# A load and three stores cut into halves of 64 partitions, and wider matmuls on zeros, in a 3x3 convolution

## The chip, the cores and the metric

The kernel runs on one core of one Trainium2 chip. The metric is device time in microseconds (us). A profile is that of a single execution; its span, from the first to the last instruction, is mostly some 1.8 us shorter than the time. A run counts as slow when it is over 1.5% above the fastest of its kernel; only fast runs are compared.

## The reference

A dense convolution, although nine tenths of the weights are zero: 16 images of 64 channels and 64x64 pixels, f32, padded by one, to 128 channels.

```python
x = randn(16, 64, 64, 64);  weight = randn(128, 64, 3, 3) * (random > 0.9)
for b, co, ci, kh, kw:
    output[b, co] += weight[co, ci, kh, kw] * x_pad[b, ci, kh:kh+64, kw:kw+64]
```

Input is 16.8 MB, output 33.6 MB.

## The kernel before

Two images form a pair: 2 x 64 channels fill the 128 partitions of one x tile. Eight pairs are computed one after the other. GpSimd issues the loads of x, which cast f32 to bf16 on the way. The first 32 rows of pair 0 come another way: SyncE loads them as f32, so that they land sooner (at 6.81 us; the cast load of the other 32 rows, issued 0.06 us later, lands at 8.75), and VectorE and ScalarE cast them. TensorE waits for these rows and does matmuls on zeros meanwhile, to keep its clock up (in head_halves, below, they end too soon, and the clock row falls to 5).

```python
x_head = o_pool.tile([128, H, W], FP32, name="o")
nc.sync.dma_start(out=x_head[:, 0:HEAD, :], in_=pair(0)[:, 0:HEAD, :])        # HEAD = 32 rows
nc.gpsimd.dma_start(out=xs[0][:, HEAD:H, :], in_=pair(0)[:, HEAD:H, :])
ident = const_pool.tile([128, 128], BF16, name="ident")
make_identity(nc, ident)
for p in range(1, EARLY):            # pairs 1 to 3, then 24 rows of pair 4
    load(p)
load(EARLY, 0, CUT)
idle_rhs = const_pool.tile([128, 128], BF16, name="idle_rhs")
def keep_busy(n):
    for _ in range(n):
        nc.tensor.matmul(idle_ps, idle_rhs, idle_rhs, start=True, stop=True)
keep_busy(27)
# ... weights cast and transposed ...
keep_busy(28)
# ...
for p in range(NP):                  # the eight pairs
    # ... matmuls, sums; a later pair's load is issued after the pair's last block ...
            if last and blk % 2 == 1:        # the last pair goes in four parts
                for n in range(2):
                    rows = slice(r0 - 16, r0 + 16)
                    nc.sync.dma_start(out=out[2 * p + n][:, rows, :], in_=o[n][:, rows, :])
        if not last:
            for n in range(2):
                nc.sync.dma_start(out=out[2 * p + n], in_=o[n])       # one image, 2 MB
```

SyncE issues all stores. Its DMAs take eight completion semaphores in turn, 0 to 7, and at the end SyncE waits for all eight in that order.

Of the kernel before, what the change touches and what calls it, by code (L numbers as in the profile page):

```python
# [8 lines left out]
FP32 = mybir.dt.float32  # L9
BF16 = mybir.dt.bfloat16  # L10
# [17 lines left out]
def kernel(  # L28
# [6 lines left out]
    nc = tc.nc  # L35
# [5 lines left out]
    HEAD = 32  # L41

    const_pool = ctx.enter_context(tc.tile_pool(name="const", bufs=1))
# [4 lines left out]
    psum_pool = ctx.enter_context(  # L48
        tc.tile_pool(name="psum", bufs=8, space=bass.MemoryType.PSUM)
    )  # L50
# [4 lines left out]
    def pair(p):  # L55
        return x[2 * p : 2 * p + 2].rearrange("n i h w -> (n i) h w")
# [2 lines left out]
    w_sb = const_pool.tile([C_OUT, C_IN * KH * KW], FP32, name="w_sb")  # L59
    nc.sync.dma_start(out=w_sb, in_=weight.rearrange("o i kh kw -> o (i kh kw)"))  # L60
    x_head = o_pool.tile([128, H, W], FP32, name="o")
    nc.sync.dma_start(out=x_head[:, 0:HEAD, :], in_=pair(0)[:, 0:HEAD, :])
    nc.gpsimd.dma_start(out=xs[0][:, HEAD:H, :], in_=pair(0)[:, HEAD:H, :])  # L63
    ident = const_pool.tile([128, 128], BF16, name="ident")
    make_identity(nc, ident)
# [1 line left out]
    def load(p, a=0, b=H):  # L67
        nc.gpsimd.dma_start(out=xs[p][:, a:b, :], in_=pair(p)[:, a:b, :])  # L68
# [6 lines left out]
    load(EARLY, 0, CUT)  # L75


    idle_rhs = const_pool.tile([128, 128], BF16, name="idle_rhs")
    nc.vector.memset(idle_rhs, 0.0)  # L79
    idle_ps = psum_pool.tile([128, 128], FP32, name="ps")  # L80

    def keep_busy(n):
        for _ in range(n):
            nc.tensor.matmul(idle_ps, idle_rhs, idle_rhs, start=True, stop=True)  # L84

    keep_busy(27)



# [8 lines left out]
    def cast_x(copy, a, b):  # L98
        copy(out=xs[0][:, a:b, :], in_=x_head[:, a:b, :])  # L99
# [24 lines left out]
    nc.vector.tensor_copy(out=wT[:, G0], in_=ps0)  # L124
    ps2 = transposed(G2)
    nc.scalar.copy(out=wT[:, G2], in_=ps2)
    keep_busy(28)
    cast_x(nc.scalar.copy, 9, 18)
    difference(G01, ps0)
    difference(G21, ps2)  # L130
# [26 lines left out]
    def direct(p, o, r0, rows):  # L157
        ps = product(
            [(xs[p], G1, r0, 1), (xs[p], G0, r0 - 1, 1), (xs[p], G2, r0 + 1, 1)], rows
        )  # L160
        nc.scalar.copy(out=o[0][:, r0 : r0 + rows, :], in_=ps[0])  # L161
        nc.vector.tensor_copy(out=o[1][:, r0 : r0 + rows, :], in_=ps[1])  # L162

    def twos(p, o, r0):
        t0 = r0 // 2
        s = s_pool.tile([128, 8, W], BF16, name="s")
        nc.gpsimd.tensor_tensor(  # L167
            out=s, in0=xs[p][:, r0 : r0 + 16 : 2, :], in1=xs[p][:, r0 + 1 : r0 + 16 : 2, :], op=ADD
        )
        shared = product([(s, G1, 0, 1)], 8)  # L170
        pc = []
        for n in range(2):
            c = p_pool.tile([128, 8, W], FP32, name="pc")
            nc.scalar.copy(out=c, in_=shared[n])  # L174
            pc.append(c)
        even = [(xs[p], G21, r0 + 1, 2), (xs[p], G0, r0 - 1, 2)]
        odd = [(xs[p], G01, r0, 2), (xs[p], G2, r0 + 2, 2)]
        for first, terms in ((r0, even), (r0 + 1, odd)):
            ps = product(terms, 8)
            for n in range(2):  # L180
                nc.vector.tensor_tensor(  # L181
                    out=o[n][:, first : r0 + 16 : 2, :], in0=ps[n], in1=pc[n], op=ADD
                )

    for p in range(NP):
        o = [o_pool.tile([C_OUT, H, W], FP32, name="o") for _ in range(2)]
        last = p == NP - 1
        for blk in range(4):
            r0 = 16 * blk
            if BLOCKS[p][blk] == "T":  # L190
                twos(p, o, r0)


                if p == 1 and blk == 3:
                    load(EARLY, CUT, H)
                elif p > 1 and blk == 3 and p + EARLY - 1 < NP:
                    load(p + EARLY - 1)
            else:
                for r, rows in ((r0, 8), (r0 + 8, 8)):
                    direct(p, o, r, rows)  # L200
            if last and blk % 2 == 1:
                for n in range(2):
                    rows = slice(r0 - 16, r0 + 16)
                    nc.sync.dma_start(out=out[2 * p + n][:, rows, :], in_=o[n][:, rows, :])
        if not last:
            for n in range(2):
                nc.sync.dma_start(out=out[2 * p + n], in_=o[n])


# [28 lines left out]
```

## Time and profile before

| | before |
|---|---|
| time | 126.42 us (126.32 to 126.64, 3 runs) |
| span of the profile | 124.7 us |
| DMA, mean of the span | 344 GB/s of bytes written; 406 GB/s of HBM traffic |
| first rows land | 6.81 us |
| TensorE begins its convolution | 7.35 us |
| first store issued | 21.83 us |
| last store's 16 shares land | 120.98 to 123.59 us |
| from the last landing to the end | 1.16 us |

All DMAs run on 16 DMA engines; each engine carries one share of a DMA, and the semaphore rises by one as each share lands. So a DMA has 16 landings, and the last of them counts: those of the last store lie between 120.98 and 123.59 us, and SyncE's wait for them ends at 123.607. A second view, the chain that ended last, shows the way to TensorE's start (start, length, what):

```profile
1.18 5.63 DMA o<-in_x_dram
6.81 0.02 issue
6.83 0.47 DVE x L99
7.30 0.04 issue
7.35 102.09 PE ps L148 x954
```

The first rows' load, a cast of 0.47 us, then TensorE without a pause.

### The profile page before, as it was taken

The page shows a single profiled execution, that of the slowest core. Times are in us where ns is not written, and L with a number is a line of the kernel's source. Part 1 is how long each engine was busy: PE and PEld are TensorE (multiplying, and loading weights), DVE is VectorE, ACT ScalarE, POOL GpSimd, SP SyncE. Part 2 cuts the span into 40 slices and gives each one's busy share as a digit, 9 for nine tenths or more (in the row PEclk, how much of TensorE's full clock was granted, in tenths as well). Part 3 has the DMA queues.
Part 4 walks back from the last instruction along what each step waited for, and adds up shares of the span by engine and source line. Part 5 has one row for each costly group of instructions (what it writes and reads, how often), then busy time and mean ns, then how long its engine had stood idle before and what let it go on. Part 6 is the DMA issues. An engine that isn't in the chain of part 4 may idle for free.

```text
span 124.7 us, 2543 instructions
## 1 busy us (share of the span) xinstructions
PE 109.0 (87%) x1030; PEld 59.5 (48%) x1030; DVE 82.3 (66%) x135; ACT 39.0 (31%) x71; POOL 41.1 (33%) x46
## 2 busy tenths in 40 slices
PE   6999999999999999999999999999999999940000
PEld 6755555555555555555555555555555555510000
DVE  0354777877787778777877787778777878870000
ACT  4545323333333333333333333333333333300000
POOL 6427343533353335333533333333333300000000
PEclk9999999999999999999999999999999999998555
DMA  4999999999999999999999999999999999999991
GB/s 127 356 225 213 215 218 213 211 400 311 350 409 410 318 297 344 436 310 323 302 433 310 318 315 423 420 449 420 426 431 420 436 426 441 415 412 420 428 381 53
DMA packets 4188, 42.93 MB, mean 344 GB/s; under 512 B 464, under 2 KB 464, under 8 KB 976
## 3 DMA queue, kind: packets, MB, share of 16 engines
q1 hardware_dynamic: 2880, 34.90, 66.6%
q0 software_dynamic: 1296, 7.86, 30.8%
q8 instruction: 8, 0.13, 0.4%
q14 instruction: 4, 0.03, 0.1%
HBM read 17.07 MB, written 33.55 MB: 406 GB/s over the span
## 4 chain that ended last, share of the span: by engine, by line
PE 82%; DMA 5%; DVE 1%; issue 1%; DVEq 0%; SPq 0%
PE ps L148 82%; DMA o<-in_x_dram 5%; DVE o L181 1%; DVEq L233 0%; DVE x L99 0%; SPq L60 0%; DVEq L181 0%
## 5 line engine op out<-in xcount | busy, mean ns | idle before, releaser
L181 DVE TENSOR_TENSOR o<-ps,pc 128x512 f32<-128x512 f32 x124 | 77.8, 686 | 22.1 <-PE ps L148 19.8
L148 PE MATMUL ps<-x,wT 64*128 64x504 bf16 (+3 forms) x780 | 88.7, 373 | 0.3 <-DVE x L99 0.3
L148 PEld LDWEIGHTS <-wT 64*128 64x128 bf16 x966 | 54.4, 94 | 48.9 <-issue 0.3
L167 POOL TENSOR_TENSOR s<-x 128x512 bf16<-128x512 bf16 x31 | 35.6, 1151 | 57.5 <-PE ps L148 43.2
L174 ACT COPY pc<-ps 128x512 f32<-128x512 f32 x62 | 33.3, 589 | 64.0 <-issue 61.8
L148 PE MATMUL ps<-s,wT 64*128 64x512 bf16 (+1 forms) x186 | 25.7, 377 | 0.0
L84 PE MATMUL ps<-idle_rhs 128*128 128x128 bf16 x55 | 4.8, 265 | 1.0 <-DVE idle_rhs L79 1.0
L84 PEld LDWEIGHTS <-idle_rhs 128*128 128x128 bf16 x55 | 4.4, 123 | 1.0 <-DVE idle_rhs L79 1.0
L68 POOL DMA_DIRECT2D x<-in_x_dram x8 | 4.4, 561 | 0.0
L103 DVE CAST w_bf<-w_sb 128x192 bf16<-128x192 f32 (+1 forms) x4 | 1.1, 346 | 2.9 <-DMA w_sb<-in_weight_dram 2.9
L162 DVE COPY o<-ps 128x512 f32<-128x512 f32 x2 | 1.4, 692 | 2.0 <-PE ps L148 2.0
L161 ACT COPY o<-ps 128x512 f32<-128x512 f32 x2 | 1.2, 586 | 2.4 <-PE ps L148 2.4
L99 ACT CAST x<-o 128x576 bf16<-128x576 f32 (+1 forms) x2 | 1.5, 804 | 0.8 <-DMA o<-in_x_dram 0.8
L99 DVE CAST x<-o 128x576 bf16<-128x576 f32 x1 | 0.5, 460 | 1.9 <-DMA o<-in_x_dram 1.9
L103 ACT ACT_TABLE_LOAD x1 | 1.3, 1283 | 0.7 <-PEq L222 0.7
L109 PE MATMUL ps<-ident,w_bf 128*128 128x128 bf16 x9 | 1.1, 296 | 0.3 <-DVE w_bf L103 0.3
L103 ACT CAST w_bf<-w_sb 128x64 bf16<-128x64 f32 (+1 forms) x2 | 0.7, 416 | 1.8 <-DMA w_sb<-in_weight_dram 1.8
L109 PEld LDWEIGHTS <-w_bf 128*128 128x128 bf16 x9 | 0.8, 128 | 0.7 <-DVE w_bf L103 0.7
L113 DVE TENSOR_TENSOR wT<-ps,wT 128x384 bf16<-128x384 f32 x2 | 1.0, 548 | 0.0
L63 POOL DMA_DIRECT2D x<-in_x_dram x1 | 0.7, 693 | 0.8 <-POOLq L222 0.8
L79 DVE MEMSET idle_rhs<- 128x64 uint32 x1 | 0.1, 112 | 0.8 <-PEq L222 0.8
L122 ACT CAST wT<-ps 128x384 bf16<-128x384 f32 x1 | 0.5, 480 | 0.4 <-PE ps L109 0.4
(8 smaller groups left out, 2.0 us busy)
## 6 DMA issues: line engine op xcount, KB each, us to landing
out_dram<-o SPq DMA_DIRECT2D x14, 2048.0 KB, 17.4
x<-in_x_dram POOLq DMA_DIRECT2D x6, 1024.0 KB, 15.8
out_dram<-o SPq DMA_DIRECT2D x4, 1024.0 KB, 11.4
o<-in_x_dram SPq DMA_DIRECT2D x1, 1024.0 KB, 5.6
x<-in_x_dram POOLq DMA_DIRECT2D x1, 640.0 KB, 14.0
x<-in_x_dram POOLq DMA_DIRECT2D x1, 512.0 KB, 7.5
x<-in_x_dram POOLq DMA_DIRECT2D x1, 384.0 KB, 24.6
w_sb<-in_weight_dram SPq DMA_DIRECT2D x1, 288.0 KB, 3.0
```

The costliest lines, as they stand in the source:

```text
L68: nc.gpsimd.dma_start(out=xs[p][:, a:b, :], in_=pair(p)[:, a:b, :])
L84: nc.tensor.matmul(idle_ps, idle_rhs, idle_rhs, start=True, stop=True)
L99: copy(out=xs[0][:, a:b, :], in_=x_head[:, a:b, :])
L103: copy(out=w_bf4[:, g, a:b, :], in_=w_v[:, k : k + b - a, :])
L109: nc.tensor.matmul(wps[:, j, :], src, ident, start=True, stop=True)
L113: nc.vector.tensor_tensor(out=wT[:, g], in0=wps, in1=wT[:, G1], op=SUB)
L148: nc.tensor.matmul(ps[n][:, lo:hi, c_lo:c_hi], tap(g, kw, n), src[q, a:b:step, c_lo + kw - 1 : c_hi + kw - 1], start=(i == 0), stop=(i == ...
L161: nc.scalar.copy(out=o[0][:, r0 : r0 + rows, :], in_=ps[0])
L162: nc.vector.tensor_copy(out=o[1][:, r0 : r0 + rows, :], in_=ps[1])
L167: nc.gpsimd.tensor_tensor(out=s, in0=xs[p][:, r0 : r0 + 16 : 2, :], in1=xs[p][:, r0 + 1 : r0 + 16 : 2, :], op=ADD)
L174: nc.scalar.copy(out=c, in_=shared[n])
L181: nc.vector.tensor_tensor(out=o[n][:, first : r0 + 16 : 2, :], in0=ps[n], in1=pc[n], op=ADD)
```

## The change

The intent: 20 DMAs leave the last store on semaphore 3, and SyncE then walks through the waits for 4 to 7. With 24 the last store has semaphore 7. The four more DMAs come from cutting one load and three stores into two halves of 64 partitions. Besides, 55 narrow matmuls on zeros become 14 wide ones.

```diff
-    nc.sync.dma_start(out=x_head[:, 0:HEAD, :], in_=pair(0)[:, 0:HEAD, :])
+    for q in (slice(0, 64), slice(64, 128)):
+        nc.sync.dma_start(out=x_head[q, 0:HEAD, :], in_=pair(0)[q, 0:HEAD, :])
...
-    idle_rhs = const_pool.tile([128, 128], BF16, name="idle_rhs")
+    idle_rhs = const_pool.tile([128, 512], BF16, name="idle_rhs")
...
-            nc.tensor.matmul(idle_ps, idle_rhs, idle_rhs, start=True, stop=True)
-    keep_busy(27)
+            nc.tensor.matmul(idle_ps, idle_rhs[:, 0:128], idle_rhs, start=True, stop=True)
+    keep_busy(7)
...
-    keep_busy(28)
+    keep_busy(7)
...
             for n in range(2):
-                nc.sync.dma_start(out=out[2 * p + n], in_=o[n])
+                for q in (slice(0, 64), slice(64, 128)) if 2 * p + n in (2, 3, 5) else (slice(0, 128),):
+                    nc.sync.dma_start(out=out[2 * p + n][q], in_=o[n][q])
```

More of the change, by code (lines that the diff above doesn't have):

```diff
@@ L75 @@
     load(EARLY, 0, CUT)
-    idle_rhs = const_pool.tile([128, 128], BF16, name="idle_rhs")
+    idle_rhs = const_pool.tile([128, 512], BF16, name="idle_rhs")
     nc.vector.memset(idle_rhs, 0.0)
-    idle_ps = psum_pool.tile([128, 128], FP32, name="ps")
+    idle_ps = psum_pool.tile([128, 512], FP32, name="ps")
     def keep_busy(n):
         for _ in range(n):
-            nc.tensor.matmul(idle_ps, idle_rhs, idle_rhs, start=True, stop=True)
-    keep_busy(27)
+            nc.tensor.matmul(idle_ps, idle_rhs[:, 0:128], idle_rhs, start=True, stop=True)
+    keep_busy(7)
     w_v = w_sb.rearrange("o (i k) -> o k i", k=KH * KW)
```

## The prediction

Its sum came to 126.2 us: the 126.42 us of before, less 0.24 us for four waits, plus 0.04 us for four small packets per engine, and 0 for the other parts. The 0 for the matmuls on zeros was my estimate. The 106 and 56 ns are the spacing, start to start, of the narrow matmuls on zeros in the two groups of before.

The first rival says that halves run at half rate, and its chance of one in four was my estimate.

> **What bounds the kernel now.** I read the page first, its second part, where each row cuts the span into 40 slices of 3.1 us.
>
> ```profile
> PE   6999999999999999999999999999999999940000
> PEclk9999999999999999999999999999999999998555
> DMA  4999999999999999999999999999999999999991
> GB/s 127 356 225 213 215 218 213 211 400 311 350 409 410 318 297 344 436 310 323 302 433 310 318 315 423 420 449 420 426 431 420 436 426 441 415 412 420 428 381 53
> ```
>
> The reader is to see that TensorE stops in slice 36, while the DMA row stays at nine tenths or more from the second slice to the last but one. The GB/s row only looks uneven. The loads cast f32 to bf16, and the row counts the bytes written; in slices with loads alone, 213 written means 426 read. Adding packets by queue from the trace, loads counted at their f32 size, gives 420 to 433 GB/s in nearly every 2.5 us from 5 us to 120 us. The one dip is 352, between 22.5 and 25 us, where the early loads run out and the first stores are just arriving. So the **16 DMA engines are the bound**, at one steady rate.
>
> Second view, busy time by stretch. The columns are stretch, length, busy us of PE, PEld, DVE, ACT and POOL with instruction counts, clock, DMA share, GB/s:
>
> ```profile
> 2.60:6.00 3.40, 3.10 (x35) 2.67 (x34) 1.14 (x4) 1.69 (x4) 2.02 (x4) 1.00 1.03 370
> 36.00:40.00 4.00, 4.00 (x40) 2.04 (x37) 3.27 (x6) 1.07 (x2) 1.40 (x2) 1.00 0.98 416
> 50.00:53.00 3.00, 3.00 (x30) 1.58 (x28) 2.27 (x4) 1.07 (x2) 1.14 (x1) 1.00 1.00 426
> 62.50:66.00 3.50, 3.50 (x36) 1.80 (x32) 2.77 (x6) 1.07 (x2) 1.14 (x1) 1.00 1.02 431
> 112.00:121.40 9.40, 0.00 (x0) 0.00 (x0) 0.00 (x0) 0.00 (x0) 0.00 (x0) 0.63 0.97 411
> ```
>
> In the last row no engine computes and the DMA engines still work off 9.4 us of stores. TensorE and VectorE could end several us later without moving the end. The first row is the load of the first rows, running alone. The other three are the stretches in which stores move with no load beside them.
>
> Third, the end. The first line is from the DMA queue's own waits (total, times, longest), the second from the stores' issue in the timeline (start, length), the last two from the instructions of the closing line, in the window after the last landing (duration min/median/max in ns, first and last start):
>
> ```profile
> SPq L233 <- DMA out_dram<-o: 10.4, 4, 3.2
> ...
> 104.96 8.05 SPq L204 DMA_DIRECT2D out_dram<-o  x4
> ...
> L233 SPq EVENT_SEMAPHORE  x5: 28/28/28, 123.6 to 123.8; - x5
> L233 SPq EVENT_SEMAPHORE  x7: 17/28/28, 123.6 to 124.7; - x7
> ```
>
> SyncE waits for the eight hardware DMA semaphores in the order 0 to 7. There are 20 hardware DMAs, numbered round, so the last four stores have semaphores 0 to 3. The last store lands at 123.59 us. The wait for semaphore 3 ends at 123.607; those for 4 to 7, satisfied for at least 9.8 us, still go by one by one at 123.666, 123.728, 123.787 and 123.849. The closing barriers then end the span at 124.745.
>
> [...] each wait shows 28 ns but they stand 60 ns apart, and 60 is what one costs. [...] No transfer in the trace of before has 64 partitions[...]. [...] (3.06 - 0.31) / 26 = 106 ns in the first group, (1.73 - 0.22) / 27 = 56 ns in the second.
>
> **The change, part by part.**
> *Count of DMAs.* One load and three stores (images 2, 3 and 5) become two each, 24 in place of 20. In the built program the last store has semaphore 7. Four waits of 60 ns leave the path after the last landing: **-0.24 us**.
> *Extra DMAs.* Four more issues of some 0.33 us lie on SyncE's queue, which is idle between stores: 0. Each DMA adds one 4-byte packet of 9 ns per engine: +0.04 us at most. The issue of a DMA waits for the DMA eight before it. The tightest is image 0's store, landed at 34.66 us, for the second half of image 5, issued near 48 us: no wait.
> *Matmuls on zeros.* 27 and 28 of 128 columns become 7 and 7 of 512: 3456 and 3584 columns against 3584 and 3584. [...] Cost 0.
> *Halves.* Bytes and packet size stay the same. If 16 engines carry a half at the rate of a whole, the cost is 0.
> Sum: 126.42 - 0.24 + 0.04 = 126.2 us.
>
> **Rivals.**
> [...] If halves run at half rate, [...] a packet takes twice its time. The first rows have eight 8 KB packets per engine, 8 x 0.309 = 2.5 us alone; halves would take 4.9, less once the cast load joins at 5.2 us, so +1 to +1.5 us on TensorE's start. There is no slack there: at 22.5 to 25 us the DMA row already lacks stores. Of the stores, the parts moved alone are 4.0 + 3.0 + 3.5 = 10.5 us, and half the rate would lose up to 5 us. Beside loads the engines alternate packets[...]. [...] Against it: engines are not in step. Landings of image 2's 16 shares spread from 45.1 to 50.2 us[...]. Also, naming images 2, 3 and 5 looks like a choice made by trial, and such a loss would have been seen. It would give +2 to +6 us, 128 to 132 us. I give it about one in four.
> *First rows land earlier.* Two smaller issues let the first half start sooner, and TensorE with it; the dip at 22.5 us, (427 - 352) / 427 x 2.5 = 0.44 us, is all there is to gain: down to 125.8 us. Against it: both halves are needed by the first cast[...].
> *Nothing is gained.* The drift of the DMA engines' finish hides 0.24 us: the last store's 16 shares land over 2.6 us (120.98 to 123.59)[...]. 126.4 us.
>
> **Range and chances.** Three quarters on the first sum and its two small rivals, 125.7 to 126.8 us; a quarter [...] from 128 us up, of which part lies within 2% (limit 128.95). Taking the middle of all that gives 126.3 us, range 125.7 to 129.2; faster by over 2% 0.02, within 2% 0.76, slower 0.22. Faster by 2% would need 2.5 us out of engines that are already full.
>
> **What would show it.** Right: after the last landing no wait for an old hardware semaphore, and about 0.9 us in place of 1.15 to the end; 16 KB packets of the split stores still 613 to 625 ns; first rows landing near 6.8 us; TensorE beginning near 7.35. Wrong: packets of 1.2 us in the split stores, a GB/s row near 215 where a half moves alone, the first rows landing past 8 us, the first store issued past 23 us. Then the time is wrong by those stretches, not by the waits.

## The result, and the profile after

The changed kernel took 138.35 us median (137.31 to 142.25, 6 runs, two of them slow), against 126.53 us for the kernel before beside it. The ratio of fast runs is **1.0897** (1.0831 to 1.0963): slower by 9%. A ratio here is the mean time of one kernel's fast runs over that of the other's in the same rounds, so not quite the ratio of the medians. The profile fell in a fast run and has a span of 135.6 us, 10.9 more than before.

The same four rows of the page, 40 slices of 3.4 us, for the changed kernel:

```profile
PE   6912999999999999999999999999999999700000
PEclk9995599999999999999999999999999999995555
DMA  4999999639999998999999999999999999999991
GB/s 138 224 253 213 220 210 221 122 140 401 279 372 314 238 249 179 319 309 302 297 350 341 292 312 394 435 433 420 420 430 440 411 435 433 425 423 416 425 379 44
```

Three things are new. TensorE stands nearly idle in slices 3 and 4 (the 1 and the 2), and its clock is at half in slices 4 and 5. The DMA row has a hole in slices 8 and 9. And in slices 14 to 16 the DMA row is full but only 179 to 249 GB/s are written. The chain that ended last, after:

```profile
1.77 10.18 DMA o<-in_x_dram
11.96 0.03 issue
...
12.05 0.47 DVE x L100
12.53 0.04 issue
12.57 103.98 PE ps L149 x954
```

The first rows land at 11.96 us, 5.15 later than before. The stores of whole images as SyncE issues them (start, length, what), before first, then after:

```profile
21.83 78.17 SPq L207 DMA_DIRECT2D out_dram<-o  x14
```

```profile
28.94 78.42 SPq L211 DMA_DIRECT2D out_dram<-o  x17
```

Busy time by stretch (stretch, length, PE, PEld, DVE, ACT, POOL, clock, DMA share, GB/s), after:

```profile
6.00:12.00 6.00, 1.43 (x6) 0.50 (x5) 0.00 (x0) 0.03 (x1) 0.00 (x0) 0.80 1.07 242
25.00:29.00 4.00, 4.00 (x41) 2.07 (x39) 3.27 (x7) 1.28 (x3) 1.26 (x2) 1.00 0.24 46
45.00:50.00 5.00, 5.00 (x50) 2.56 (x48) 3.52 (x7) 1.91 (x4) 2.16 (x2) 1.00 1.05 239
```

The last two of these stretches, before:

```profile
25.00:29.00 4.00, 4.00 (x41) 2.10 (x38) 2.96 (x5) 1.83 (x4) 1.90 (x2) 1.00 1.02 396
45.00:50.00 5.00, 5.00 (x50) 2.68 (x48) 3.94 (x7) 1.29 (x3) 2.06 (x3) 1.00 1.02 329
```

Between 25 and 29 us the DMA engines are now busy for 24%: the early loads run out and the first store is issued only at 28.94 us. From 45 to 50 us little but the two halves of image 2 moves (they land by 48.60 and 55.15 us), and the engines look full (1.05) at 239 GB/s. (The 329 of before are no full rate either way: a load moves there too, and its bytes count half: the page has 7.86 MB for the cast loads' 15.7 MB of f32.) By the records of single packets, 16 KB packets that took 0.611 to 0.624 us before take 1.27 us there at the median; 11 of the 73 still take less than 0.7.

A balance by 2.5 us stretches, HBM bytes against before in each and a steady 427 GB/s, puts the loss at 1.3 us up to 10 us, 3.7 us less 0.4 for the old dip between 22.5 and 30, 0.8 from 30 to 37.5, and 5.2 from there to 80: 10.6 of the 10.9 us. Of the 5.2 us, 4.3 lie between 42.5 and 55 us, while image 2 moves; images 3 and 5, which move beside loads, lose little.

The end is as intended. The closing line's instructions in the window from 134.6 to 135 us, around the last landing (134.69 us), after:

```profile
L237 SPq EVENT_SEMAPHORE  x2: 17/22/28, 134.7 to 135.0; - x2
```

One wait and the barrier's, where before had five waits in a row. From the last landing to the end are 0.91 us in place of 1.16.

### The profile page after: what moved, and what is told of

Same layout as the page of the kernel before. It is cut to its first block, busy times and chain, and to the rows that moved or that the text cites. A ratio compares the mean times of both kernels' runs of the same rounds, so it can differ in the third digit from the quotient of the medians.

```text
span 135.6 us, 2472 instructions
## 1 busy us (share of the span) xinstructions
PE 111.4 (82%) x989; PEld 56.3 (41%) x989; DVE 82.4 (61%) x135; ACT 39.0 (29%) x71; POOL 41.2 (30%) x46
## 3 DMA queue, kind: packets, MB, share of 16 engines
q0 software_dynamic: 1296, 7.86, 28.1%
## 4 chain that ended last, share of the span: by engine, by line
PE 77%; DMA 8%; DVE 1%; SPq 1%; issue 1%; DVEq 0%
PE ps L149 77%; DMA o<-in_x_dram 8%; DVE o L182 1%; DVEq L237 0%; SPq L63 0%; DVE x L100 0%; SPq L60 0%; DVEq L100 0%; DVEq L182 0%
## 5 line engine op out<-in xcount | busy, mean ns | idle before, releaser
L149 PE MATMUL ps<-x,wT 64*128 64x504 bf16 (+3 forms) x780 | 90.5, 379 | 5.1 <-DVE x L100 5.1
L149 PEld LDWEIGHTS <-wT 64*128 64x128 bf16 x966 | 53.8, 95 | 56.6 <-issue 7.8
L85 PE MATMUL ps<-idle_rhs 128*128 128x512 bf16 x14 | 5.3, 541 | 1.2 <-DVE idle_rhs L80 1.2
L85 PEld LDWEIGHTS <-idle_rhs 128*128 128x128 bf16 x14 | 1.7, 132 | 3.5 <-issue 1.9
## 6 DMA issues: line engine op xcount, KB each, us to landing
x<-in_x_dram POOLq DMA_DIRECT2D x1, 512.0 KB, 10.5
```

Of the source, the lines that this page charges most:

```text
L85: nc.tensor.matmul(idle_ps, idle_rhs[:, 0:128], idle_rhs, start=True, stop=True)
L149: nc.tensor.matmul(ps[n][:, lo:hi, c_lo:c_hi], tap(g, kw, n), src[q, a:b:step, c_lo + kw - 1 : c_hi + kw - 1], start=(i == 0), stop=(i == ...
```

## The experiments

My theory after the result, "half rate" below: a transfer of partitions 0 to 63 or 64 to 127 alone moves at about half the rate, as image 2's halves did (239 GB/s where 427 are full). It makes the first rows late, which starts TensorE and so the stores late, and it slows the stores. Rivals: each extra DMA costs by itself; or the wide matmuls let the clock fall. "Mean" below is that of the fast runs.

| run | what | mean, us | beside it, before | ratio (95%) |
|---|---|---|---|---|
| head_halves | first rows in halves | 132.33 | 126.49 | 1.0461 (1.0415 to 1.0508) |
| store_halves | images 2, 3, 5 in halves | 132.0 (2 fast of 4) | 126.49 | none given; 1.044 by division |
| wide_only | wide matmuls | 126.98 | 126.49 | 1.0038 (0.9999 to 1.0077) |
| rows_24 | the whole change, but cut by rows | 131.99 | 126.49 | 1.0435 (1.0397 to 1.0472) |
| store_middle | images 2, 3, 5 in 64 + 32 + 32 | 131.75 | 126.43 | 1.0406 (1.0368 to 1.0443) |
| store_late | images 10, 11, 13 in halves | 140.0 (2 fast of 4) | 126.43 | 1.1074 (1.1049 to 1.1099) |
| store_rows_24 | images 2, 3, 5, 7 by rows | 127.15 | 126.43 | 1.0057 (1.0035 to 1.0079) |
| head_halves_warm | head_halves, clock held up | 130.38 | 126.43 | 1.0313 (1.0287 to 1.0339) |
| tail_quarters, tail_quarters_b | last pair in eight stores | 126.52, 126.42 | 126.70, 126.51 | 0.9986 (0.9944 to 1.0029), 0.9993 (0.998 to 1.0006) |
| identity_first | first cast load 0.2 us later | 126.54 | 126.51 | 1.0002 (0.9988 to 1.0016) |
| identity_quarters | both of the last two | 126.54 | 126.51 | 1.0001 (0.9987 to 1.0014) |
| late_whole, late_halves, late_rows | looks at the first rows alone | one run each | | |

All results were correct.

### The parts one by one: head_halves, store_halves, wide_only

head_halves takes the first hunk of the change alone:

```diff
-    nc.sync.dma_start(out=x_head[:, 0:HEAD, :], in_=pair(0)[:, 0:HEAD, :])
+    for q in (slice(0, 64), slice(64, 128)):
+        nc.sync.dma_start(out=x_head[q, 0:HEAD, :], in_=pair(0)[q, 0:HEAD, :])
```

> The kernel before with only the first rows' load in two halves of 64 partitions (21 hardware DMAs). [...] the rows land near 12 us in place of 6.8, TensorE idles some 5 us and its clock falls, the first store goes near 29 us in place of 21.8, and the DMA engines stand idle for some 4 us between 25 and 29 us: 131 to 132 us. Rival, cost of each extra DMA: one more DMA costs a quarter of the whole loss at most, under 129.5 us. Rival, the wide matmuls are to blame: 126.4 us here.

It cost 5.8 us, a little over half of the whole loss. The rows landed at 12.20 us and the first store went at 29.65. Page row of the clock, and the stretch of the hole, in head_halves:

```profile
PEclk9996589999999999999999999999999999999855
...
25.00:29.00 4.00, 4.00 (x40) 2.06 (x38) 3.27 (x7) 1.07 (x2) 1.15 (x1) 1.00 0.27 53
```

The matmuls on zeros are narrow here and the clock falls all the same, so they are not what lets it fall. The hole of 4 us is the same as in the changed kernel. A single extra DMA takes half of the loss, so the loss doesn't go by the count.

store_halves takes the last hunk alone:

```diff
-                nc.sync.dma_start(out=out[2 * p + n], in_=o[n])
+                for q in (slice(0, 64), slice(64, 128)) if 2 * p + n in (2, 3, 5) else (slice(0, 128),):
+                    nc.sync.dma_start(out=out[2 * p + n][q], in_=o[n][q])
```

> The kernel before with only the stores of images 2, 3 and 5 in halves of 64 partitions (23 hardware DMAs). [...] their packets take 1.2 us in place of 0.61 where no load runs beside them, 427 GB/s fall to some 210 there, and 5 to 7 us are lost: 131 to 133 us. First rows and first store as before (6.8 and 21.8 us). Rival, cost of each extra DMA: three more, packets of 0.61 to 0.63 us with gaps between the DMAs.

Its two fast runs took 131.58 and 132.43 us; two were slow, so no interval. The loss of 5.5 us is as expected, and it adds up: 5.8 + 5.5 = 11.3 us, where the changed kernel lost 137.85 - 126.5 = 11.35 in the means. The start is as before (rows 6.77, first store 21.79). One stretch, before first, then store_halves:

```profile
37.50:42.50 5.00, 5.00 (x50) 2.62 (x48) 3.55 (x7) 2.15 (x4) 2.29 (x2) 1.00 1.02 377
```

```profile
37.50:42.50 5.00, 5.00 (x50) 2.63 (x46) 3.54 (x7) 2.15 (x4) 2.29 (x2) 1.00 1.03 305
```

The engines are as busy and write a fifth less. Something else shows at the end: the last store's shares land over 5.3 us (124.30 to 129.59), where they need 2.6 before. Some engines are done long before the others. On average the 16 shares land 3.9 us later than before, and the last one lags this average by 2.1 us more; so the 5.5 us are not lost rate alone, and their fit with the expectation is in part luck.

wide_only takes the middle hunks alone:

```diff
-    keep_busy(27)
+    keep_busy(7)
...
-    keep_busy(28)
+    keep_busy(7)
```

with the tile of zeros 512 columns wide in place of 128, as in the change.

> The kernel before with only the matmuls on zeros made wide (7 and 7 of 512 columns). My theory: not on the path, 126.4 us within 0.2. Rival: TensorE's clock rises about 1 us later, or falls again, the first store is issued later than 21.8 us by 0.5 us or more, and the time rises by as much.

Its median is 126.66 us and its profile's span 124.7, to the tenth that of before; first store 21.89 us. Two of six runs lie at 127.5 and 128.05 and pull the ratio up. No cost is shown. The rival is refuted: the clock rose at 4.1 us and stayed.

### The same cuts by rows: rows_24, and what it taught

```diff
-    for q in (slice(0, 64), slice(64, 128)):
-        nc.sync.dma_start(out=x_head[q, 0:HEAD, :], in_=pair(0)[q, 0:HEAD, :])
+    for a in (0, 16):
+        nc.sync.dma_start(out=x_head[:, a : a + 16, :], in_=pair(0)[:, a : a + 16, :])
...
-                for q in (slice(0, 64), slice(64, 128)) if 2 * p + n in (2, 3, 5) else (slice(0, 128),):
-                    nc.sync.dma_start(out=out[2 * p + n][q], in_=o[n][q])
+                for r in (slice(0, 32), slice(32, 64)) if 2 * p + n in (2, 3, 5) else (slice(0, H),):
+                    nc.sync.dma_start(out=out[2 * p + n][:, r, :], in_=o[n][:, r, :])
```

> The changed kernel with the same five loads and stores cut, but by image rows, so that each part still has 128 partitions; 24 hardware DMAs, last store on the last semaphore. [...] nothing is lost, the four waits of 60 ns are gone from the end, 126.2 us (0.2 under the kernel before, 0.05 to 0.3 allowed). Rival, cost of each extra DMA: as slow as the changed kernel, 135 us or more, or at least some us slower than before.

This was a clear miss: 1.0435, although every part has 128 partitions. Half rate for parts of 64 partitions doesn't explain the loss alone. The trace says where it came from. The stores do well: their 8 KB packets take 0.309 us where they are alone, and 418 to 424 GB/s move there (56 to 58 and 43 to 47 us). The first rows don't: the first part lands at 5.79 us, the second at 13.05. The chain that ended last in rows_24:

```profile
1.63 11.42 DMA o<-in_x_dram
```

The packet records show why the second part is late. The packets of the cast loads on the other queue begin at 4.6 us, when about half of the first rows' packets are still to come. For a microsecond the loads lead (44 of their packets begin from 5.5 to 6.5 us, 14 of the first rows). Then an engine takes one packet of each queue in turn: 0.172 us for 4 KB of the first rows, 0.322 us for 4 KB (8 KB of f32) of pair 0, later 0.624 us for 8 KB of pair 1. Late packets of the first rows show it: they begin at 9.671, 10.444, 11.216 and 11.989 us, about one small and one large packet apart. So the first rows, in smaller packets, get a third of the engines' time or less. In the kernel before, the first rows are nearly through when the loads arrive at 5.2 us: 111 of their 128 packets have begun. It is a **race**, and I had left it out.

What sets the arrival of the loads is not shown. GpSimd issues the first of them at 1.24 us in these kernels (1.43 in the two identity runs; the late runs, below, are another matter). Its packets begin at 5.1 to 5.4 us in every such profile in which the first rows are one load, but at 3.25 us in head_halves, 3.67 in the changed kernel and 4.6 in rows_24 and head_halves_warm. So a cut of the first rows does not only delay them: the others also join earlier.

### The first rows alone: late_whole, late_halves, late_rows

Ten memsets on GpSimd ahead of its first load take the other side out of the race. These kernels are slower on purpose; only landings are read.

```diff
-    nc.gpsimd.dma_start(out=xs[0][:, HEAD:H, :], in_=pair(0)[:, HEAD:H, :])
     ident = const_pool.tile([128, 128], BF16, name="ident")
     make_identity(nc, ident)
+    delay = const_pool.tile([128, 512], BF16, name="delay")
+    for _ in range(10):
+        nc.gpsimd.memset(delay, 0.0)
+    nc.gpsimd.dma_start(out=xs[0][:, HEAD:H, :], in_=pair(0)[:, HEAD:H, :])
```

late_halves and late_rows add the cut of the first rows of head_halves and of rows_24.

> A control, slower on purpose: the kernel before with GpSimd's first loads held back by ten memsets, so that nothing runs beside the first rows' load. All theories: whole, the rows land near 6.8 us as before; the loads begin past 8 us.

> The control with the first rows' load in two halves of 64 partitions. If the halves' lateness (12.0 us in place of 6.8) is mostly the alternation with the cast loads: the second half lands near 8 to 8.5 us here[...]. If [...] the second DMA itself cost all of it: still 11 to 12 us.

> The control with the first rows' load in two parts of 16 rows, 128 partitions each. If alternation with the loads made the second part land at 13 us: here near 7 to 8 us. If a second DMA on the queue is late in itself: still 10 us or more.

The time from issue to landing, in late_whole, late_halves and late_rows (with two DMAs, the last of the three numbers counts):

```profile
DMA to landing us min/median/max: 5.2/5.2/5.2
```

```profile
DMA to landing us min/median/max: 5.5/6.3/7.1
```

```profile
DMA to landing us min/median/max: 4.5/4.9/5.3
```

| first rows land, us | whole | halves | rows |
|---|---|---|---|
| loads held back | 6.38 | 8.80 | 6.93 |
| loads as usual | 6.81 | 12.20 | 13.05 |

Without loads beside them, rows cost 0.55 us and halves 2.42. The estimate for half rate was 1 MB in 4.9 us in place of 2.5: 2.4 more. Most packets of the second half took 0.55 to 0.65 us against 0.309. So for the first rows by themselves half the rate is measured, in one profile of each kernel. In late_halves TensorE stood still for 2.07 us (7.34 to 9.41), and its clock fell to half at 9.36 us, for 3.4 us. With the loads, halves lose 5.4 us (12.20 - 6.81): 2.4 at half the rate, and by difference 3.0 from the lost race. Here the first cast load is issued at 7.0 to 7.3 us, and its packets begin only at 8.4 to 8.7, after the last of the rows'. In late_whole the balance puts a loss of 3.8 us between 5 and 10 us, most of what it is slower by.

### How much of it is the clock: head_halves_warm

```diff
-    keep_busy(28)
+    keep_busy(28 + 90)
```

on top of head_halves.

> The kernel with the first rows' load in halves, and 90 more narrow matmuls on zeros (5 us) that fill the gap in which TensorE waits for the rows. If the fallen clock is a part of the loss: the clock stays whole, the first store is issued near 27.7 us in place of 29.65, and the time falls by 1.5 to 2 us, from 132.5 to some 130.5. Rival, the clock doesn't matter because the DMA engines are the bound anyway: 132.5 us as without.

The mean is 130.38 us, 1.95 under head_halves, as expected; the two ran in different sets, each against its own runs of before (1.0461 and 1.0313). The clock stays up until the end and the first store goes at 27.38 us. Page row of the clock in head_halves_warm:

```profile
PEclk9999999999999999999999999999999999999655
```

So of the 5.8 us that the halves of the first rows cost, some 2 come by way of TensorE's clock. TensorE is not the bound, but it sets when the first store can go, and the early loads are used up by then.

### Which partitions a store covers: store_middle, store_late

```diff
+                for q in (slice(32, 96), slice(0, 32), slice(96, 128)) if 2 * p + n in (2, 3, 5) else (slice(0, 128),):
+                    nc.sync.dma_start(out=out[2 * p + n][q], in_=o[n][q])
```

> The kernel before with the stores of images 2, 3 and 5 in three parts: partitions 32 to 95, 0 to 31, 96 to 127. [...] the first part has 64 partitions, as a half has[...]; its packets stay at 0.61 to 0.63 us. The two parts of 32 partitions [...] take about 1.2 us a packet where no load runs beside them. About half of what the halves lost (5.4 us) is lost: 128 to 130 us. Rival, any DMA of fewer than 128 partitions is slow, or each extra DMA costs: as slow as the halves or slower, 132 us or more, and the packets of the middle part slow too.

The time missed my range: 131.75 us, as slow as the halves. The packets bear out half of the theory. I had expected full rate for partitions 32 to 95, which lie on both sides of 64, and half rate for the two parts of 32, each on one side. Two stretches of store_middle:

```profile
50.00:52.00 2.00, 2.00 (x22) 1.03 (x18) 1.27 (x3) 1.07 (x2) 1.14 (x1) 1.00 1.06 418
52.00:55.00 3.00, 3.00 (x30) 1.60 (x28) 2.38 (x4) 1.08 (x2) 1.13 (x1) 1.00 0.97 240
```

In the first mostly the middle part of image 3 moves (it lands from 50.3 to 53.4 us): 46 of 51 packets take 0.61 to 0.67 us and 418 GB/s move, with 64 partitions. In the second come the parts of 32: 15 of 39 packets take 1.0 to 2.2 us, and 240 GB/s move. So it isn't the number of partitions as such, nor the 1 MB that such a part has in HBM: it is which partitions a part covers. The reason for it is not shown. That the parts of 32 take up to 2.2 us, and not 1.2, I can't explain; the packets carry no mark of their DMA, and I assign them by the order of the queue. The last store's shares end 6.1 us apart.

store_late cuts three images that move when no load is left (against store_halves):

```diff
-  ... if 2 * p + n in (2, 3, 5) else ...
+  ... if 2 * p + n in (10, 11, 13) else ...
```

> The kernel before with the stores of images 10, 11 and 13 in halves of 64 partitions, which move when no load is left. [...] here nothing hides it, the packets all take 1.2 to 1.3 us, each image costs some 4.9 us more than the 4.9 it takes whole, 12 to 15 us in all: 138 to 142 us. If the loads beside them had hidden nothing in the kernel with images 2, 3 and 5, the loss would be the same as there, 5.4 us: 132 us.

("It" is the loss by half rate, of which loads beside the stores may hide a part.) It lost 13.6 us at a ratio of 1.1074, near the 14.7 us of three images at half rate (but see below), and two and a half times what images 2, 3 and 5 lost. So loads beside the stores do hide more than half of it. The traffic of the stretch in question, before first, then store_late:

```profile
92.00:110.00 18.00, 18.00 (x172) 9.47 (x168) 13.79 (x23) 6.44 (x12) 3.46 (x3) 1.00 1.01 427
```

```profile
92.00:120.00 28.00, 18.71 (x176) 9.67 (x172) 15.86 (x26) 6.44 (x12) 3.46 (x3) 0.89 1.00 316
```

Not all packets take twice their time: some 60% of them keep 0.61 to 0.7 us, others mostly take 1.0 to 1.5. The landings tell what that means. The first share of each of the four halves of images 10 and 11 lands at 94.21, 96.63, 99.07 and 101.94 us: one every 2.4 to 2.9 us, near the full rate. The last share lands at 97.34, 101.18, 104.89 and 110.09: one every 3.7 to 5.2. The engines don't share equally. Some run ahead at full rate, others fall behind, and a store is done when the slowest is. The last store's shares land from 124.71 to 136.91 us, 12.2 us apart. Which engines these are the trace doesn't say.

The 16 landings of the last store split each loss in two: the rate that all engines lost, and the lag of the slowest.

| | mean of the 16 landings, us | last landing after the mean, us |
|---|---|---|
| before | 122.18 | 1.41 |
| store_halves | 126.04 | 3.55 |
| store_middle | 125.31 | 3.94 |
| store_late | 130.28 | 6.63 |

These are single profiles. In store_late 8.1 us are lost rate and 5.2 are lag. So the nearness to 14.7 us, which is for half the rate and no lag, is in part luck. In store_middle 3.1 us are lost rate, four fifths of the 3.9 of store_halves where I had expected half, and 2.5 us are lag.

### The intent without the halves: store_rows_24, tail_quarters, identity_first, identity_quarters

If only the last semaphore mattered, other cuts should gain 0.24 us. store_rows_24 leaves the first rows whole and cuts four images by rows, as rows_24 does:

```diff
+                for r in (slice(0, 32), slice(32, 64)) if 2 * p + n in (2, 3, 5, 7) else (slice(0, H),):
+                    nc.sync.dma_start(out=out[2 * p + n][:, r, :], in_=o[n][:, r, :])
```

> The kernel before with the first rows' load whole, and the stores of images 2, 3, 5 and 7 cut by rows into two parts of 128 partitions: 24 hardware DMAs, the last store on the last semaphore. After the last run I hold that all of its loss came from the cut of the first rows' load, none from the stores. So here: no loss, and the four waits of 60 ns gone from the end: 126.1 to 126.4 us. Rival, cost of each extra DMA in the stores: 128 us or more.

It missed: 1.0057, slower by 0.7 us (within 2%, but the interval lies above 1). The end is short (0.90 us), but the last share landed at 124.89 us in place of 123.59, with the shares 3.4 us apart. Cutting these stores by rows is almost free, not free; I don't know what moves the engines apart here.

tail_quarters cuts the last pair's stores into eight parts in place of four:

```diff
-            if last and blk % 2 == 1:
+            if last:
                 for n in range(2):
-                    rows = slice(r0 - 16, r0 + 16)
+                    rows = slice(r0, r0 + 16)
```

> The kernel before with the stores of the last pair in eight parts of 16 rows in place of four of 32, 24 hardware DMAs, so that the last store has the last semaphore by another way. No wait of 60 ns behind the last landing: -0.24 us; packets of 4 KB move at 96% of the rate (159 ns for 4 KB against 309 for 8 KB), 4.2 MB of them, +0.3 us at most. 126.2 to 126.6 us. If semaphores count for more than 60 ns each: under 126.

> The eight smaller last stores again, whose profile fell in the slow state the first time. In a fast profile: last landing to end 0.9 us in place of 1.15, last landing near 123.5 us, time 126.2 to 126.5 us. If its slow executions come from the first rows losing the race to the cast loads: a fast profile has them landing near 6.8 us, where the slow one had 11.3.

(The 159 ns for 4 KB are near an estimate from the trace of before: 309 ns for 8 KB and 611 for 16 KB give 158.) 0.9986 the first time (0.9944 to 1.0029), 0.9993 the second (0.998 to 1.0006): 126.42 us against 126.51, a gain of 0.1 us that isn't clear of noise. The profile of the second run has 0.90 us from the last landing to the end, and the last landing at 123.71, 0.12 later than before. Half of the 0.25 us went into the later landing. The profile of the first fell in a slow run, in which the first rows, whole, landed at 11.29 us. Fifteen of their 16 shares landed by 6.93; one engine alone had its last six packets 0.62 us apart, in turn with those of the loads. So the race can be lost without a cut, by one engine.

identity_first issues the first cast load after the identity matrix; identity_quarters adds the cut of tail_quarters.

```diff
-    nc.gpsimd.dma_start(out=xs[0][:, HEAD:H, :], in_=pair(0)[:, HEAD:H, :])
     ident = const_pool.tile([128, 128], BF16, name="ident")
     make_identity(nc, ident)
+    nc.gpsimd.dma_start(out=xs[0][:, HEAD:H, :], in_=pair(0)[:, HEAD:H, :])
```

> The kernel before with GpSimd's first cast load issued after the identity matrix in place of before it, some 0.6 us later. In the runs so far the first rows land near 6.8 us when their packets are done before the cast loads arrive (5.2 us), and at 11 to 13 us when even a part is left by then, whole load or not. If that race is the cause: the rows still land by 6.9 us, all executions stay fast, and the time is 126.3 to 126.8 us. If the position of this load is no matter: 126.5 with the odd execution near 131.7, as before.

> The same, and the last pair's stores in eight parts of 16 rows, so that the last of 24 hardware DMAs has the last semaphore. If the 0.24 us of four waits is a gain of its own: 0.1 to 0.3 us under the run with the identity first. If the engines' uneven finish hides it: the same.

Both took the time of before (1.0002 and 1.0001). The load moved by only 0.2 us, from 1.24 to 1.43, less than the 0.6 I had counted on. All their runs were fast, but so were the eleven of before beside them: whether this makes the race safer is left open. No version here beats the kernel before by more than noise.

The length of the end, though, follows the count of waits in every fast profile:

| satisfied waits behind the last store | run | last landing to end, us |
|---|---|---|
| 0 | changed kernel, tail_quarters_b | 0.91, 0.90 |
| 1 | store_halves | 0.97 |
| 3 | head_halves | 1.08 |
| 4 | before, wide_only | 1.16, 1.14 |
| 6 | store_middle | 1.28 |

That is 0.06 us for each wait, as the prediction had it from the kernel before.

## Why the prediction was wrong

The prediction gave 126.3 us and a range of 125.7 to 129.2; 137.85 us, the mean of the fast runs, lies far outside. Point by point:

- **What bounds the kernel: right.** The 16 DMA engines at 427 GB/s. Every loss found is either time in which they stood idle or time in which they moved less.
- **Count of DMAs, -0.24 us: right as a term**, shown by the table of waits. As a gain it was not fully realised in any run.
- **Extra DMAs, 0: near enough.** store_rows_24 has four more and lost 0.7 us, although its end is 0.25 us shorter. (In the changed kernel the cut stores took SyncE 0.5 to 2.6 us to issue and not 0.33, at no cost that shows.)
- **Matmuls on zeros, 0: right** (wide_only). But "TensorE and VectorE could end several us later without moving the end" holds for delay at the end alone: the tail of 9.4 us covers none at the first store. head_halves_warm puts the cost of the fallen clock at 2 us.
- **"Halves. If 16 engines carry a half at the rate of a whole, the cost is 0": this step failed**, and the sum with it. In late_halves packets of the first rows took 0.55 to 0.65 us in place of 0.309, and in the changed kernel the halves of image 2 moved at 239 GB/s where 427 are full. The two cuts alone cost 5.8 us (head_halves) and 5.5 us (store_halves). (The trace of before has 611 to 624 ns for the packets that the prediction gives as 613 to 625.)
- **The rival "If halves run at half rate" was right in kind, but its size and its chance were wrong.** Its 128 to 132 us end 6 us short. Its term for the first rows, "+1 to +1.5 us on TensorE's start", measured 5.2 us (7.35 to 12.57). I took the cast loads that join at 5.2 us for a help. They joined at 3.67 us, and they are what makes the rows so late, since the engines take turns by packet (seen in rows_24): 2.4 us at half the rate, some 2.8 more from the race. TensorE then ran at half its clock until 16.4 us, which cost another 1.9, and the first store went 7.1 us late (21.83 to 28.94). I didn't turn "there is no slack there" into idle DMA time, which was 3.7 us. Its term for the stores, "up to 5 us", came near the 5.5 us of store_halves, in part by luck: the lost rate was 3.9 us in its profile, and the lag of the slowest engine, 2.1 us, which the term leaves out, came on top. It also halved stretches of fixed length, 10.5 us, as if the bytes left over then moved beside loads for nothing; without loads, in store_late, the loss was 13.6 us. (And the stretch from 36 us on is not of cut stores alone: image 1, whole, lands at 38.0 us and after.)
- **The chance, one in four.** It rested on two arguments. The first, that "engines are not in step", was misread: of image 2's 16 shares 13 land within 1.3 us (45.1 to 46.4), and two alone at 50.2. In store_late some 60% of the packets do keep 0.61 to 0.7 us, but the slowest engine ends the kernel, 6.63 us after the mean of the 16. The second, that "naming images 2, 3 and 5 looks like a choice made by trial", is an argument about the author and not about the trace. Neither measures a transfer of 64 partitions, and no trace that I had then shows one: one in four was an estimate.

Three things stay open. In the changed kernel, head_halves, head_halves_warm and rows_24, packets of the two first stores, which are whole, take 0.74 to 1.17 us for a while near 34 us (0.8 us lost in the changed kernel); before doesn't show it. Which engines run ahead when halves move isn't shown. Nor is what lets the loads join earlier when the first rows are cut: how many of their packets are left then doesn't decide alone, since 17 were left before (rows at 6.81 us) and 16 in the slow run of tail_quarters (11.29 us).

## What to carry to other kernels

Before a change adds DMAs, look at which SBUF partitions each part covers: cutting along partitions can halve the rate of a transfer, and a DMA row that looks full doesn't show it (1.05 at 239 GB/s here), so compare GB/s and the time of one packet. A load that the whole start waits for can win only because it is nearly done when others join (here 111 of its 128 packets had begun). A cut of it can cost far more than the cut's own time: by rows this was 0.55 us alone and 6.2 us beside the loads, which joined earlier and then shared the engines packet by packet. A gain of 0.2 us behind the last landing is worth having only if nothing upstream moves by as much.
